# Gate products by rows of tokens: each contraction of 128 rows as two of 64, in two banks

## The chip, the cores and the metric

The kernel runs on one core of one Trainium2 chip. A core has a matrix engine (TensorE, PE in the profile, with its weight loads as PEld), a vector engine (VectorE, DVE), a scalar engine (ScalarE, ACT), GpSimd (POOL), and SyncE (SP), which issues most of the transfers. Products go into PSUM, whose banks hold 512 F32 numbers on each of 128 partitions; everything else lies in SBUF. The metric is the device time of one execution in microseconds. The kernel before takes 1186.93 us, the median of three runs (1186.53 to 1187.04).

## The reference

Two layers over 256 tokens of width 1024. Each has a SwiGLU block, a mixer, and a second SwiGLU block, all with a residual and a layer norm. The change is in the mixer, in the two gates; cut to that:

```python
def _mixer(x, layer, w_in, gate_b, ...):
    z = x @ w_in
    u, v, q, k, val, gates = jnp.split(z, SPLITS, axis=-1)
    h_a = _chunked_sgu(gelu(u), gelu(v), ...)
    h_b = _diff_attention(rope(q), rope(k), val, lam_full)      # with a norm behind it
    g = jax.nn.sigmoid(gates.reshape(bsz, seq, N_BRANCH, D_MODEL) + gate_b)
    m = g[:, :, 0] * (h_a @ w_branch[0]) + g[:, :, 1] * (h_b @ w_branch[1])
    return m @ w_out
```

For each branch the gate is a product of 256 tokens with a 1024 x 1024 matrix, plus a bias, through a sigmoid. Half of its columns (512) are made by rows of tokens, which is the part that changes; the other half by columns of the gate.

## The kernel before, in words

Precision. Inputs and weights are F32. Each product is made of three in a shorter form (fp32r): a number is split into hi and lo, and hi·hi, lo·hi and hi·lo are added up in a bank. ACT makes the hi of a weight (L195), DVE the lo (L197), in `stream`, which also fetches 1 MB of weights; buffers for hi and lo number eight each. `xh` and `xl` are the two parts of x, transposed, so that the contraction lies on the partitions: KT = 8 blocks of 128 rows.

A gate by rows of tokens (`gate_rows`, L1103) calls `gemm_b` (L324). That takes one bank for each half of the tokens (t = 0 and 1, 128 tokens each). With `tail=TAIL` = 8 all four weight pieces are held, and the products run t by t: for each t, eight blocks k, and for each the three products of `three` (L280, its matmuls are on L283): the weight load is a block of x (128 x 128), the moving operand 512 columns of the weight. That is 24 products for each t. When a t is through, `done` adds the bias into `gr` (DVE, L1109) and takes the tanh (ACT, L1110).

A gate by columns (`gate_columns`, L1114) and the q and k products (`rope`, L968) call `gemm_a2` (L285): two banks, eight products of 512 columns for each on L295, then eight of 256 columns for each on L302; ACT copies half of each bank (L303) and DVE adds the other half to it (L305, or L307 for q), which frees the bank.

Banks. PSUM is a pool of four "main" banks and four "side" banks. A main bank is taken from the four in turn, by `bank()`; a product into it waits until the last reader of its former content is through.

Order. TensorE's order is written out by hand: it executes exactly in the order of the code. The other engines' instructions are put in order by a scheduler that goes by priorities. Work beside the products (attention, norms) is a set of small tasks; `beat(w)` moves a clock on after so many products, and a task whose time has come adds its instructions there. So attention's products stand between those of the gates: the scores (`scores`, L1001, F32, with 64 rows each, in two banks in turn) and the product with the values (L1055 and L1057, F32, 128 rows). The scores pass through DVE (L1013) and ACT's exponential (L1015).

In each layer the order around the change is: q and k of four pairs of heads, gate rows of branch 0 (stage 1 below), gate columns of branch 0, gate rows of branch 1 (stage 2), gate columns of branch 1, and so on.

Of the kernel before, what the change touches and what calls it, by code (L numbers as in the profile page):

```python
# [17 lines left out]
ALU = mybir.AluOpType  # L18
AX = mybir.AxisListType

P = 128
D = 1024
T = 256
NT = T // P
KT = D // P
# [14 lines left out]
TAIL = 8  # L40
# [14 lines left out]
def trunk(ctx, tc, x, xT, w13a, w13b, w2, wb, wqk, wu, wg, wgr, wbr, wbrr, wo, gateb, gatebr, sgug, sgub, sguwT, sgubias, lam, diffg,  # L55
          lng, lnb, lngT, lnbT, cosT, sinT, out):
    nc = tc.nc
    V, A, G, PE = nc.vector, nc.scalar, nc.gpsimd, nc.tensor
# [15 lines left out]
    def name(s):  # L74
        serial[0] += 1
        return f"{s}_{serial[0]}"

    def bank():
        return psum.tile([P, 512], F32, tag="main", name=name("bank"))

    def side_bank():
        return psum.tile([P, 512], F32, tag="side", name=name("sbank"))

    def slots(s, n, dtype=F32):

        return [act.tile([P, 512], dtype, tag="slot", name=name(s)) for _ in range((n + 1) // 2)]
# [8 lines left out]
    def parts(f):  # L95
        return (lambda k: f(k)[:, :T]), (lambda k: f(k)[:, T:])
# [27 lines left out]
    def beat(w):  # L124

        clock[0] += w
        for task in list(tasks):
            if task[0] <= clock[0]:
                turn(task)

    def turn(task):
        try:
            task[0] = clock[0] + next(task[1])
        except StopIteration:
            tasks.remove(task)
# [10 lines left out]
    latest, added, emptied, silu, turned_by, loaded, spread = [None, None], [None], [None], [None], [None], [None], [None]  # L146
# [3 lines left out]
    def inline(eng, ins):  # L150
        if line[2]:
            line[eng is V] = ins
        return ins

    def behind(ins):

        return tc.issue_after(ins) if ins is not None else nullcontext()

    def fetch(src, width=CH, raw=None):

        step()
        if raw is None:
            raw = raw_pool.tile([P, CH], F32, tag="raw", name=name("raw"))
        for g in gate:
            g[0] -= 1
        while len(gate) > 1 and gate[1][0] < 0:
            gate.pop(0)
        with behind(gate[0][1] if gate and gate[0][0] < 0 else None):
            if isinstance(raw, list):
                for j, v in enumerate(raw):  # L170
                    loaded[0] = nc.sync.dma_start(v, src[:, j * HC : (j + 1) * HC]).ins
            else:
                loaded[0] = nc.sync.dma_start(raw[:, :width], src).ins
        return raw

    def stream(src, width=CH, sub=HC, lent=(), after=(None, None), pool=()):

        raw = fetch(src, width)  # L180
        out = []
        first = sooner.pop() if sooner else latest
        for o in range(0, width, HC):
            eng = G if o // HC in pool else V
            if o // HC in lent:
                hi, lo = ([act.tile([P, 512], F32R, tag="slot", name=name(n)) for _ in range(2)] for n in ("lhi", "llo"))
                at = [(hi[j], lo[j]) for j in range(2)]
            else:
                hi = hi_pool.tile([P, HC], F32R, tag="hi", name=name("whi"))
                lo = lo_pool.tile([P, HC], F32R, tag="lo", name=name("wlo"))  # L190
                at = [(hi[:, p : p + sub], lo[:, p : p + sub]) for p in range(0, HC, sub)]
            for p, (h, w) in zip(range(0, HC, sub), at):
                r = raw[:, o + p : o + p + sub]
                with behind(first[0]), behind(line[0]):
                    inline(A, A.activation(h, r, AF.Copy).ins)  # L195
                with behind(after[o // HC] or (first[1] if eng is V else None)), behind(line[1] if eng is V else None):
                    low = eng.tensor_tensor(out=w, in0=r, in1=h.bitcast(F32), op=ALU.subtract).ins  # L197
                if eng is V:
                    inline(V, low)
            out.append((hi, lo))  # L200
        return out
# [112 lines left out]
    def rows_b(ps, t, k0, piece, xh, xl, kts, c0=0, n=512, first=0):  # L314

        hi, lo = piece
        for j in range(2):
            k, o = k0 + j, j * 512 + c0
            wh, wl = (w[j][:, c0 : c0 + n] if isinstance(w, list) else w[:, o : o + n] for w in (hi, lo))
            three(ps[:, :n], xh(k)[:, t * P : (t + 1) * P], xl(k)[:, t * P : (t + 1) * P], wh, wl,  # L320
                  k == first, k == (first - 1) % kts)
        beat(n / 1024)

    def gemm_b(src, kts, xh, xl, done, tail=4, last=()):  # L324

        blocks = [[(bank(), c, n) for c, n in (last if t else ()) or ((0, 512),)] for t in range(NT)]
        held = []
        for c in range(0, kts, 4):
            nk = min(4, kts - c)
            for i, piece in enumerate(stream(src[:, c * 512 : (c + nk) * 512], nk * 512)):  # L330
                k = c + 2 * i
                if k >= kts - tail:
                    held.append((k, piece))
                    continue
                for t in range(NT):
                    for ps, o, n in blocks[t]:
                        rows_b(ps, t, k, piece, xh, xl, kts, o, n)
        for t in range(NT):
            for ps, o, n in blocks[t]:
                for k, piece in held:  # L340
                    rows_b(ps, t, k, piece, xh, xl, kts, o, n)
                done(t, ps[:, :n], o, n)

    def homes(pool, tag):
        return [pool.tile([P, HC], F32, tag=tag, name=name("home")) for _ in range(2)]
# [191 lines left out]
    b = side_bank()  # L537
# [47 lines left out]
    def bc_load(src, after):  # L585
        t = res.tile([P, D], F32, tag="bc", name=name("bc"), bufs=2)
        V.tensor_copy(t[:, :1], after)
        spread[0] = G.dma_start(t, src.partition_broadcast(P)).ins
        return t
# [363 lines left out]
    def mixer(l, i, norm):  # L953
        xh, xl = parts(both)
# [139 lines left out]
        for hp in range(HEADS // 2):  # L1094
# [3 lines left out]
            if hp == 1:  # L1098
                gbias = bc_load(gatebr[l], qT[:, :1])
# [3 lines left out]
        def gate_rows(br):  # L1103

            gr = [slots("gr", 2)[0] for _ in range(NT)]
            grow.append(gr)

            def done(t, ps, c, n):
                added[0] = V.tensor_tensor(out=gr[t], in0=ps, in1=gbias[:, br * 512 : (br + 1) * 512], op=ALU.add).ins  # L1109
                emptied[0] = A.activation(gr[t], gr[t], AF.Tanh, scale=0.5).ins  # L1110

            gemm_b(wgr[l, br, 0], KT, xh, xl, done, tail=TAIL)

        def gate_columns(br):  # L1114
            gt = slots("gate", KT // 2)
# [7 lines left out]
        for br in range(2):  # L1123
            gate_rows(br)
            gate_columns(br)
# [14 lines left out]
        for h in range(2):  # L1140
            def got_v(t, ps, c, n):
                A.activation(vg[t][:, h], ps, AF.Gelu)
                V.bn_stats(out=vst[t][:, h * 6 : h * 6 + 6], in_=vg[t][:, h])
            gemm_b(wb[l, V_, h], KT, xh, xl, got_v)
# [14 lines left out]
        for h in range(2):  # L1159
            s = slice(h * 512, h * 512 + 512)  # L1160
# [34 lines left out]
        def branch_rows(br, h):  # L1195
            def done(t, ps, c, n):
                g = grow[br][t]
                a = V.scalar_tensor_tensor(out=g, in0=g, scalar=1.0, in1=ps, op0=ALU.add, op1=ALU.mult)
                if br == 0:
                    a = V.tensor_tensor(out=g, in0=g, in1=grow[1][t], op=ALU.add)  # L1200
                    beside(turned(t, g, grow[1][t]), 0)
                added[0] = a.ins

            gemm_b(wbrr[l, br, 0], KT, lambda k: h[k][:, :T], lambda k: h[k][:, T:], done, tail=8)
# [137 lines left out]
```

## Time and profile before

| what | value |
|---|---|
| median of three runs | 1186.93 us |
| the profiled execution, own time | 1186.92 us |
| its span | 1185.2 us |
| TensorE's granted clock, mean | 1.0 |
| gate stages, layer 0: start, end | 250.15 to 262.41 us, 275.23 to 289.22 us |
| gate stages, layer 1: start, end | 836.56 to 848.83 us, 861.64 to 875.63 us |

The rows of the profile read like this. In the timeline a row is: start in us from the span's start, how long, engine, line, operation, output <- inputs, shapes (for PE rows x columns of the weights, then the moving operand), how often in a row, and in brackets idle time before it with what ended it. A product's listed length includes its way through the array, so lengths overlap; steps are read from starts. A row with "x8" covers eight products from the first start to the last end. A row of one line's or one tile's instructions has shortest/median/longest in ns. L numbers are lines of the kernel before, as printed above.

### The profile page before, as it was taken

To read this page: it belongs to the slowest core of one execution; us is meant where nothing else is said; L and a number is where in the kernel's file an instruction comes from. 1 tells how busy PE (TensorE), PEld (TensorE's weight loads), DVE (VectorE), ACT (ScalarE), POOL (GpSimd) and SP (SyncE) were. 2 spreads that over 40 slices of the span, in tenths; PEclk is the share of its full clock that TensorE was granted. 3 is DMA by queue.
4 is the path that set the end of the run, shared out by engine and by line. 5 is a ranking of instruction groups with operands and counts; after the bars stand their busy time and mean duration, and the time that the engine had idled before them with its cause. 6 is when DMAs were issued, how large, how long until landed. Compare 5 with 4: busy or idle time off the path is not lost.

```text
span 1185.2 us, 16670 instructions
## 1 busy us (share of the span) xinstructions
PE 1179.9 (100%) x5775; PEld 993.9 (84%) x5775; DVE 1012.7 (85%) x1562; ACT 827.7 (70%) x1417; POOL 287.1 (24%) x350
## 2 busy tenths in 40 slices
PE   9999999999999999999999999999999999999998
PEld 7888888888888888888888888888888888888887
DVE  6989989788688989889899889888975989988895
ACT  6688658559955677876667876576798556679761
POOL 1012201247420220051020171003564112102600
PEclk9999999999999999999999999999999999999999
DMA  9869976768865658689668699586666755786881
GB/s 355 261 203 262 288 273 209 262 194 236 247 208 170 227 190 272 186 275 275 231 222 263 191 278 274 201 290 226 212 213 205 254 182 170 253 251 206 274 258 36
DMA packets 129620, 275.10 MB, mean 232 GB/s; under 512 B 89040, under 2 KB 90368, under 8 KB 105472
## 3 DMA queue, kind: packets, MB, share of 16 engines
q1 hardware_dynamic: 121968, 248.67, 63.4%
q0 software_dynamic: 6992, 24.71, 8.7%
q8 instruction: 45, 0.74, 0.2%
q10 hardware_dynamic: 576, 0.66, 0.2%
q14 instruction: 39, 0.32, 0.1%
HBM read 248.05 MB, written 1.05 MB: 210 GB/s over the span
## 4 chain that ended last, share of the span: by engine, by line
PE 99%; DMA 0%; DVE 0%; ACT 0%; DVEq 0%; issue 0%
PE bank L283 46%; PE bank L295 15%; PE sbank L376 12%; PE bank L410 10%; PE bank L302 8%; PE sbank L410 3%; PE bank L527 2%; PE sbank L1001 1%; PE bank L376 1%; PE sbank L1057 1%; PE sbank L1175 1%; DMA xtok<-in_xT 0%; PE sbank L1055 0%; PE sbank L698 0%; DVE xtok L685 0%; DVE st L635 0%
## 5 line engine op out<-in xcount | busy, mean ns | idle before, releaser
L197 DVE TENSOR_TENSOR wlo<-raw,whi 128x1024 fp32r<-128x1024 f32 (+1 forms) x346 | 379.2, 1123 | 50.5 <-ACT whi L195 36.6
L195 ACT ACTIVATE whi<-raw 128x1024 fp32r<-128x1024 f32 (+1 forms) x350 | 323.4, 952 | 131.6 <-PE bank L283 42.7
L283 PE MATMUL bank<-whi,x 128*128 128x512 f32 x1224 | 386.3, 390 | 0.0
L283 PEld LDWEIGHTS bank<-whi,x 128*128 128x128 f32 x1224 | 229.8, 188 | 47.6
L283 PE MATMUL bank<-wlo,x 128*128 128x512 f32 x612 | 238.2, 389 | 0.0
L249 DVE TENSOR_TENSOR wlo<-raw,whi 128x1024 fp32r<-128x1024 f32 (+1 forms) x123 | 143.3, 1186 | 21.7 <-ACT whi L247 12.8
L247 ACT ACTIVATE whi<-raw 128x1024 fp32r<-128x1024 f32 (+1 forms) x123 | 121.1, 1002 | 53.7 <-DVE raw L359 24.8
L295 PE MATMUL bank<-x,whi 128*128 128x512 f32 x640 | 153.3, 391 | 0.0
L295 PEld LDWEIGHTS bank<-x,whi 128*128 128x128 f32 x640 | 118.2, 188 | 23.8
L283 PEld LDWEIGHTS bank<-wlo,x 128*128 128x128 f32 x612 | 114.9, 188 | 23.4
L229 POOL COPY seven<-seven 128x512 uint16<-128x512 uint16 x16 | 58.6, 3722 | 134.2 <-ACT whi L195 54.7
L302 PEld LDWEIGHTS bank<-x,wlo 128*128 128x128 f32 x640 | 81.4, 191 | 2.9
L302 PE MATMUL bank<-x,wlo 128*128 128x256 f32 x640 | 82.6, 283 | 0.0
L410 PE MATMUL bank<-whi,hhi 128*128 128x512 f32 (+1 forms) x182 | 68.2, 375 | 0.0
L410 PE MATMUL bank<-whi,hlo 128*128 128x512 f32 (+1 forms) x182 | 67.9, 373 | 0.0
L410 PE MATMUL bank<-wlo,hhi 128*128 128x512 f32 (+1 forms) x182 | 67.9, 373 | 0.0
L977 POOL TENSOR_TENSOR swap<-swap,sin_t 128x512 f32<-128x512 f32 x16 | 27.3, 1704 | 101.4 <-DMA swap<-z 69.7
L741 POOL COPY nvia<-ntwo 128x256 uint16<-128x256 uint16 x20 | 9.8, 539 | 162.2 <-DMA ntwo<-nvia 156.1
L303 ACT ACTIVATE r<-bank 128x256 f32<-128x256 f32 x96 | 34.8, 372 | 16.7 <-PE bank L302 16.7
L376 PE MATMUL sbank<-whi,xhs 128*128 128x512 f32 x128 | 42.0, 389 | 0.0
L359 DVE TENSOR_TENSOR raw<-raw,home 128x1024 f32<-128x1024 f32 x32 | 39.1, 1235 | 1.7 <-DMA home<-in_w13b 1.7
L410 PEld LDWEIGHTS bank<-whi,hlo 128*128 128x128 f32 x182 | 34.3, 188 | 6.1
(285 smaller groups left out, 2150.0 us busy)
## 6 DMA issues: line engine op xcount, KB each, us to landing
raw<-in_w13b SPq DMA_DIRECT2D x68, 1024.0 KB, 6.0
raw<-in_w SPq DMA_DIRECT2D x32, 1024.0 KB, 7.1
raw<-in_wb SPq DMA_DIRECT2D x16, 1024.0 KB, 6.0
raw<-in_wqk SPq DMA_DIRECT2D x16, 1024.0 KB, 6.4
home<-in_w13b SPq DMA_DIRECT2D x16, 512.0 KB, 5.9
raw<-in_w13a SPq DMA_DIRECT2D x8, 1024.0 KB, 4.9
home<-in_w SPq DMA_DIRECT2D x16, 512.0 KB, 4.2
raw<-in_wgr SPq DMA_DIRECT2D x8, 1024.0 KB, 5.3
```

The source lines that it names most:

```text
L195: inline(A, A.activation(h, r, AF.Copy).ins)
L197: low = eng.tensor_tensor(out=w, in0=r, in1=h.bitcast(F32), op=ALU.subtract).ins
L229: eng.tensor_copy(out=o, in_=i)
L247: a = A.activation(hi, src, AF.Copy).ins
L249: return a, eng.tensor_tensor(out=lo, in0=src, in1=hi.bitcast(F32), op=ALU.subtract).ins
L283: PE.matmul(ps, xx, w, start=start and n == 0, stop=stop and n == 2)
L295: PE.matmul(b[-1], hi[:, k * P : (k + 1) * P], xc(k), start=k == 0, stop=False)
L302: PE.matmul(b[n][:, :T], lo[:, k * P : (k + 1) * P], xc(k)[:, :T], start=False, stop=k == KT - 1)
L303: emptied[0] = A.activation(r[:, s], b[n][:, T:], AF.Copy, scale=scale).ins
L359: inline(V, V.tensor_tensor(out=v, in0=v, in1=m, op=ALU.add).ins)
L376: PE.matmul(ps, x[o](k), y, start=start and k == n == 0, stop=stop and k == 3 and n == 2, skip_group_check=True)
L410: PE.matmul(q[c][t][:, :n] if o == 0 else more[:, :n], x(k, t), y, start=k == 8 and m == 0 and (c, t) != (1, 0), stop=k == FT - 1 and m == ...
```

## The change

`gate_rows` calls a new function, `gemm_halves`, in place of `gemm_b`. Each product of 128 rows becomes two: rows 0-63 of x and of the weight go into one bank, rows 64-127 into another, one behind the other in TensorE's order. So a stage has four banks, two for each t, and 96 products in place of 48. DVE's `done` adds the bias to the first bank, then the second bank to that. The weights, their splits and the transfers are the same. (Blank lines at the head of the new function are left out.)

```diff
+    def gemm_halves(src, xh, xl, done):
+        ps = [[bank() for _ in range(2)] for _ in range(NT)]
+        held = [piece for c in range(0, KT, 4) for piece in stream(src[:, c * 512 : (c + 4) * 512])]
+        for t in range(NT):
+            for n, (hi, lo) in enumerate(held):
+                for j in range(2):
+                    k, s = 2 * n + j, slice(j * 512, (j + 1) * 512)
+                    xs_ = [x(k)[:, t * P : (t + 1) * P] for x in (xh, xl)]
+                    for m, (w, x) in enumerate(((hi, xs_[0]), (lo, xs_[0]), (hi, xs_[1]))):
+                        for half, b in enumerate(ps[t]):
+                            r = slice(half * P // 2, (half + 1) * P // 2)
+                            PE.matmul(b, x[r], w[r, s], start=k == m == 0, stop=k == KT - 1 and m == 2)
+                beat(0.5)
+            done(t, ps[t])
...
-            def done(t, ps, c, n):
-                added[0] = V.tensor_tensor(out=gr[t], in0=ps, in1=gbias[:, br * 512 : (br + 1) * 512], op=ALU.add).ins
+            def done(t, ps):
+                V.tensor_tensor(out=gr[t], in0=ps[0], in1=gbias[:, br * 512 : (br + 1) * 512], op=ALU.add)
+                added[0] = V.tensor_tensor(out=gr[t], in0=gr[t], in1=ps[1], op=ALU.add).ins
                 emptied[0] = A.activation(gr[t], gr[t], AF.Tanh, scale=0.5).ins
 
-            gemm_b(wgr[l, br, 0], KT, xh, xl, done, tail=TAIL)
+            gemm_halves(wgr[l, br, 0], xh, xl, done)
```

The order of instructions moves with it. TensorE, layer 0, stage 1, where t=0 ends and t=1 begins, before (buffer numbers are kept; banks are handed out in the order of these numbers, 2400 and 2445 being the last k product's, the two just ahead of the stage; what an instruction waits for is in brackets, DVE_49 being VectorE):

```order
L283 MATMUL bank_480_2494<-whi_490_2512,x_216_1213 128x512
L283 MATMUL bank_480_2494<-wlo_491_2513,x_216_1213 128x512
L283 MATMUL bank_480_2494<-whi_490_2512,x_216_1213 128x512 x2
L283 MATMUL bank_480_2494<-wlo_491_2513,x_216_1213 128x512
L283 MATMUL bank_480_2494<-whi_490_2512,x_216_1213 128x512
L283 MATMUL bank_481_2495<-whi_483_2498,x_215_1212 128x512 [waits DVE_49]
L283 MATMUL bank_481_2495<-wlo_484_2499,x_215_1212 128x512
```

and now:

```order
L360 MATMUL bank_480_2494<-whi_492_2514,x_216_1213 128x512
L360 MATMUL bank_481_2495<-whi_492_2514,x_216_1213 128x512
L360 MATMUL bank_482_2496<-whi_485_2500,x_215_1212 128x512 [waits DVE_49]
L360 MATMUL bank_483_2497<-whi_485_2500,x_215_1212 128x512 [waits DVE_49]
L360 MATMUL bank_482_2496<-wlo_486_2501,x_215_1212 128x512
L360 MATMUL bank_483_2497<-wlo_486_2501,x_215_1212 128x512
```

Before, t=0 and t=1 take the banks of the k product before the last (2341 and 2350), and the last k product's two go to the gate columns behind the stage. Now t=0 takes both of the former, and t=1 the two banks of the last k product, 2400 and 2445, whose reader on VectorE is the row z<-bank (L305). Elsewhere TensorE's order is the same, the visits of the attention included: L1055 and L1057 within t=1 of stage 1, and between t=0 and t=1 of stage 2; the scores (L1001) in the middle of t=1 of stage 2.

VectorE in the same place, before (z is the k product's sum, qk its rotated form, gr the gate):

```order
L305 TENSOR_TENSOR z_472_2455<-bank_470_2445,r_471_2454 128x256 [waits Activation_49]
L1032 RECIPROCAL rc_461_2412<-sums_459_2410 128x4
L197 TENSOR_TENSOR wlo_531_2715<-raw_527_2708,whi_530_2714 128x1024
L1033 SCALAR_TENSOR_TENSOR c_460_2411<-rc_461_2412,neg_lam0_1894,sums_459_2410 128x4 [waits DVE_49]
L1024 SCALAR_TENSOR_TENSOR d_473_2479<-pp_467_2430,c_460_2411,pp_466_2425 128x256 [waits DVE_49]
L1024 SCALAR_TENSOR_TENSOR d_473_2479<-pp_467_2430,c_460_2411,pp_466_2425 128x256
L1024 SCALAR_TENSOR_TENSOR d_474_2480<-pp_469_2440,c_460_2411,pp_468_2435 128x128 x2
L976 TENSOR_TENSOR qk_477_2487<-z_472_2455,cos_t_137 128x512
L1109 TENSOR_TENSOR gr_478_2492<-bank_480_2494,bc_403_2165 128x512 [waits DMASW7_49,PE_49]
L981 TENSOR_TENSOR qk_477_2487<-qk_477_2487,swap_476_2486 128x512 [waits DMAHW4_49,DMAHW5_49,DVE_49,Pool_49]
```

and now:

```order
L996 TENSOR_TENSOR qk_477_2487<-z_472_2455,cos_t_137 128x512
L1001 TENSOR_TENSOR qk_477_2487<-qk_477_2487,swap_476_2486 128x512 [waits DMAHW4_49,DMAHW5_49,DVE_49,Pool_49]
L1129 TENSOR_TENSOR gr_478_2492<-bank_480_2494,bc_403_2165 128x512 [waits DMASW7_49,PE_49]
L1130 TENSOR_TENSOR gr_478_2492<-gr_478_2492,bank_481_2495 128x512 [waits DVE_49,PE_49]
L197 TENSOR_TENSOR wlo_549_2834<-raw_547_2831,whi_548_2833 128x1024 [waits DMAHW3_49,Activation_49]
L197 TENSOR_TENSOR wlo_551_2838<-raw_547_2831,whi_550_2837 128x1024 [waits Activation_49]
```

The rows up to the first qk row are the same as before. The two adds of t=0 stand behind the second qk row, where the one add stood ahead of it. In stage 2 two weight splits on VectorE stand further ahead, one of them before the scores' rows and one between the two adds of t=1; the rest of VectorE's order is the same, and ScalarE's, GpSimd's and SyncE's differ in a place or two each in stage 2 or not at all.

## The prediction, as it was put on record

> **What bounds the kernel now.** I read the page's busy times and its chain first, then TensorE's own list of waits.
>
> ```profile
> PE 1179.9 (100%) x5775; PEld 993.9 (84%) x5775; DVE 1012.7 (85%) x1562; ACT 827.7 (70%) x1417; POOL 287.1 (24%) x350
> PE 99%; DMA 0%; DVE 0%; ACT 0%; DVEq 0%; issue 0%
> PE sbank L539 <- DVE warm L535: 1.1, 1, 1.1
> PE sbank L677 <- ACT minus L675: 0.7, 1, 0.7
> PE bank L527 <- ACT x L247: 0.3, 1, 0.3
> ```
>
> TensorE (PE) is the bound from end to end: 99% of the chain is PE, and its waits are three, 2.1 us in all (columns: us in total, times, longest), none of them near the gates. So what the change adds to PE's sequence goes straight into the time, and a new wait of PE is paid in full: there is no other wait that it could replace. What counts is the step from one product to the next, read from starts in the timeline of the first gate stage (layer 0, branch 0):
>
> ```profile
> 252.45 0.39 PE L283 MATMUL bank<-wlo,x 128*128 128x512 f32 x1
> 252.67 0.61 PE L283 MATMUL bank<-whi,x 128*128 128x512 f32 x2
> 253.13 0.39 PE L283 MATMUL bank<-wlo,x 128*128 128x512 f32 x1
> ```
>
> Three products in 0.68 us are 0.2267 us each, though each is listed as 0.39 (they overlap). A gate stage is 48 of them, 24 for each half of the tokens (t=0, then t=1), and there are four stages, two in each layer: 192 products, which become 192 pairs.
>
> **The pair itself: 0, with bounds.** The kernel already has pairs of 64 rows in two banks: the attention's scores (L1001, F32).
>
> ```profile
> 226.67 0.60 PE L1001 MATMUL sbank<-qk,qk 64*128 64x256 f32 x4
> 226.89 0.60 PE L1001 MATMUL sbank<-qk,qk 64*128 64x256 f32 x4
> 227.10 0.60 PE L1001 MATMUL sbank<-qk,qk 64*128 64x256 f32 x6
> 227.32 0.50 PE L1001 MATMUL sbank<-qk,qk 64*128 64x128 f32 x6
> 259.70 0.38 PE L1055 MATMUL sbank<-val,d 128*128 128x128 f32 x2
> 259.92 0.61 PE L1057 MATMUL sbank<-val,aT 128*128 128x128 f32 x4
> 260.37 0.39 PE L1055 MATMUL sbank<-val,d 128*128 128x128 f32 x2
> ```
>
> Pairs of 256 columns start every 0.217 us (226.67 to 227.32 in three steps), 0.108 per 128 columns. Full-height F32 products of 128 columns take 0.112 (0.45 us for the four from 259.92 to 260.37). So two halves side by side cost one whole product: they do run together, and they gain nothing either, because the columns still pass one after another. The gates' products are of the faster form (fp32r), for which no pair is in the trace. Its bounds: 256 columns take 0.1195 (1.91 us for the sixteen L302 rows below, 248.24 to 250.15), so 512 columns are 0.2145 and 0.012 is a gap per product (2 x 0.1195 - 0.2267). If the pair loses the gap it steps by 0.2145, if it has it twice by 0.239. I take 0.2267, since the F32 rows show a pair stepping like a single product.
>
> **Passing between heights: +2.3 us.**
>
> ```profile
> 242.85 2.00 PE L295 MATMUL bank<-x,whi 128*128 128x512 f32 x8
> 244.78 1.58 PE L1001 MATMUL sbank<-qk,qk 64*128 64x256 f32 x16
> 246.29 2.11 PE L295 MATMUL bank<-x,whi 128*128 128x512 f32 x8
> 248.24 2.08 PE L302 MATMUL bank<-x,wlo 128*128 128x256 f32 x16
> 250.15 0.40 PE L283 MATMUL bank<-whi,x 128*128 128x512 f32 x1
> 260.95 0.48 PE L283 MATMUL bank<-whi,x 128*128 128x512 f32 x1
> 262.41 0.39 PE L295 MATMUL bank<-x,whi 128*128 128x512 f32 x1
> ```
>
> Around one visit to 64 rows: eight products take 1.93 instead of 8 x 0.2267 = 1.81, the scores 1.51 instead of 4 x 0.217 + 4 x 0.108 = 1.30, the next eight 1.95 instead of 1.81. That is 0.12 + 0.21 + 0.14 = 0.47, say 0.23 each way. The visit to L1055/L1057, F32 at full height, costs nothing: its twelve products take 1.25 (259.70 to 260.95; 12 x 0.112 = 1.34) and the six behind 1.46 (6 x 0.2267 = 1.36). So the price belongs to the height, not to the type. The Trainium skill (TensorEngine Tiling (Array Packing), Key Properties) says that a change of the tiling mode, though not of the tile, drains TensorE. The trace agrees, by the 0.47; without that rule the sum below would be 2.8.
>
> Passages per layer in the new order: in (stage 1), out and in around L1055/L1057, out; in (stage 2), out and in around L1055/L1057, out: 8. The scores inside stage 2 now stand among 64-row pairs, so their 2 passages go. The first "in" is swallowed by the wait below. 8 - 2 - 1 = 5, times 0.23, times 2 layers = 2.3. Bounds: 0 if fp32r hides them, 3.5 if each is half as dear again.
>
> **The bank wait: +2.8 us.** Four accumulating banks are handed out in turn. Before, a stage took two; the two behind them stayed with the last q/k product (L295/L302) until VectorE (DVE) had read them. Now t=1 needs exactly those two, and the DVE row that frees the second stands at:
>
> ```profile
> 255.42 0.39 ACT L1015 ACTIVATE pp<-pp,mx 128x128 f32<-128x128 f32 x1
> 255.81 0.36 ACT L303 ACTIVATE r<-bank 128x256 f32<-128x256 f32 x1
> 256.07 1.04 ACT L195 ACTIVATE whi<-raw 128x1024 fp32r<-128x1024 f32 x1
> 257.02 0.35 ACT L303 ACTIVATE r<-bank 128x256 f32<-128x256 f32 x1
> 257.41 0.42 DVE L305 TENSOR_TENSOR z<-bank,r 128x256 f32<-128x256 f32 x1 [0.19 <-ACT r L303]
> 255.39 0.61 PE L283 MATMUL bank<-whi,x 128*128 128x512 f32 x2
> 836.56 0.40 PE L283 MATMUL bank<-whi,x 128*128 128x512 f32 x1
> 841.80 0.62 PE L283 MATMUL bank<-whi,x 128*128 128x512 f32 x2
> 842.18 0.42 DVE L305 TENSOR_TENSOR z<-bank,r 128x256 f32<-128x256 f32 x1 [0.19 <-ACT r L303]
> ```
>
> Layer 0: t=1 starts at 255.62 (second product of the 255.39 row, 5.47 after 250.15); the bank is free at 257.41 + 0.42 = 257.83: PE is 2.21 late. Layer 1: start 842.03, bank free 842.60: 0.57. Together 2.8. Nothing in the change moves that DVE row: it waits for ScalarE (ACT), whose copy stands behind the softmax exponentials (L1015) and a weight split, all fed before the stage. PE is in order, so while it waits all products of t=1 and the whole rest stand behind it. A slower or faster t=0 changes nothing here while it ends before the bank is free.
>
> In the second stage of a layer t=1 takes the banks of the gate columns before it, and these are read (L305, gz) long before; after the first wait PE is later still.
>
> **The adds on DVE: 0.** Eight more adds; the nearest row, the first add, has 0.684 each:
>
> ```profile
> L1109 DVE TENSOR_TENSOR gr<-bank,bc x8: 677/684/692, 261.1 to 876.5; 128x512 f32<-128x512 f32 x8
> 262.39 1.07 DVE L981 TENSOR_TENSOR qk<-qk,swap 128x512 f32<-128x512 f32 x1 [0.59 <-POOL swap L977]
> 847.15 1.07 DVE L981 TENSOR_TENSOR qk<-qk,swap 128x512 f32<-128x512 f32 x1 [0.57 <-POOL swap L977]
> 848.83 1.52 PE L295 MATMUL bank<-x,whi 128*128 128x512 f32 x6
> ```
>
> What hides them is PE's new lateness. The gate columns behind stage 1 take t=0's banks, and both adds of t=0 now stand behind the q/k add: in layer 1 they free the first bank at 847.15 + 1.07 + 0.68 = 848.90 and the second at 849.58. PE wants the first at 848.83 + 0.57 + 0.46 + 0.23 = 850.09: 1.2 us of cover (layer 0: 264.14 against 262.41 + 2.21 + 0.69 = 265.31, also 1.2). Without it, the first add alone would cost up to 0.7 a layer.
>
> **Sum:** 0 + 2.3 + 2.8 + 0 = +5.1 us on the profiled execution, whose own time is 1186.92 (span 1185.2 and 1.7 around it); the median is 1186.93. Forecast **1192.0**. With the pair's bounds on the 144 products that no wait covers (24 + 48 per layer): 144 x 0.012 = 1.7 either way, and about 1.1 for the passages: 1189 to 1195.
>
> **Rivals.** (1) The halves share a way to the banks. In the F32 rows each half delivers a column in twice the time that an fp32r product needs (0.217 for 256 columns against 0.2267 for 512), so two full-rate streams side by side have not been seen. If they took turns altogether, a pair would be 0.4533: 192 x 0.2267 = 43.5, the bank wait gone (t=0 ends late enough), 6 passages a layer, 2.8: 1233. If a pair were a tenth dearer, 0.249: 144 x 0.0227 = 3.3, and t=0 in layer 1 ends 0.2 past its bank: 1195.5. Against it: F32 pairs show no trace of sharing. The Trainium skill (TensorE: Matmul & The Clock Gate, Measured speedup vs the span model) has 3.07 instead of 4 for four row tiles of 512 columns; as an estimate from that, two would cost about 1.1 of one, the second of these cases. No run here shows it yet.
>
> (2) Not slower: the banks are free in time. The place is the DVE row of the last q/k product, the price 2.8. It decides from the point where that row ends before 255.8 in layer 0, 2 us sooner; between the layers its lead over PE does differ by 1.6 (7.68 after the stage's start against 6.04). Then two more "in" are paid: 5.1 - 2.8 + 0.5 = 2.8 at 0.2267 a pair, 0.5 with the gap lost on all 192 (-2.3). Middle: 1.7, 1188.6. Against it: nothing upstream changes.
>
> (3) Faster would need a pair under 0.2145 - the columns forbid that - or waits that I do not see in PE's list.
>
> **Numbers.** Forecast 0.74, rival 1 0.13, rival 2 0.08, faster 0.05. This kernel's measurement tells 0.2% (2.4 us) from no change; so slower 0.87, same 0.08, faster 0.05. The range runs from rival 2's middle, 1188.5, to 1196.5, past the tenth-dearer pair; it leaves out the serial pair and the faster cases.
>
> **What will show it.** Two starts 5 to 10 ns apart in each pair and 0.227 between pairs; a PE wait of some 2.2 us at 255.6 with DVE z as its releaser, and of 0.3 to 0.6 in layer 1; products at each change of height some 0.1 us late; no PE wait at the gate columns. Pairs of 0.45, no wait at t=1, or a wait for the gr adds would prove me wrong.

## The result, and the profile after

| | before | after |
|---|---|---|
| median | 1186.73 us (1186.46 to 1187.04, 4 runs) | 1194.58 us (1194.31 to 1195.86, 4 runs) |
| ratio, 95% interval | | 1.0067 (1.0054 to 1.0079) |
| profiled execution, own time and span | 1186.92 us, 1185.2 us | 1194.31 us, 1192.6 us |
| granted clock, mean | 1.0 | 1.0 |

The change costs 7.85 us by the medians and 7.4 by the two spans. The page after the change, its busy times and its chain's first line:

```profile
PE 1184.5 (99%) x5967; PEld 995.5 (83%) x5967; DVE 1016.2 (85%) x1570; ACT 828.0 (69%) x1417; POOL 285.4 (24%) x350
PE 92%; DVE 3%; ACT 2%; issue 1%; POOL 1%; DMA 0%; SPq 0%; DVEq 0%; POOLq 0%; ACTq 0%
```

TensorE is nearly as full as before (99% of the span busy against 100%), and still only 92% of the chain is TensorE, where it was 99%: 5% now runs through VectorE and ScalarE. So somewhere TensorE waits for a chain of those two. TensorE's own list of waits says where (us in total, times, longest):

```profile
PE sbank L1075 <- ACT d L1069: 1.8, 2, 0.9
PE bank L360 <- DVE z L305: 1.3, 2, 0.7
PE sbank L559 <- DVE warm L555: 1.0, 1, 1.0
PE sbank L697 <- ACT minus L695: 0.7, 1, 0.7
```

The last two are those of before (1.1 and 0.7). The second is the bank wait, as forecast. The first is new and in no term of the prediction: the values product (L1075, before L1055) waits for ScalarE's d.

How much each place costs is read by taking the same product of TensorE in both traces and subtracting the starts. Where this difference grows, time is lost. It is -0.20 us ahead of the first gate stage (the heads of the two executions differ by that) and 7.43 at the end, so the change loses 7.63:

| stretch | layer 0 | layer 1 |
|---|---|---|
| stage 1 | 2.91 | 0.81 |
| stage 2 and up to the values product in the u part | 0.86 | 0.65 |
| the values product in the u part | 1.13 | 1.14 |
| what is left, up to the next layer or the end | 0.11 | 0.02 |

TensorE's timeline of the changed kernel where t=1 of stage 1 begins in layer 0, with VectorE's rows that free the two banks:

```profile
254.71 0.62 PE L360 MATMUL bank<-whi,x 64*128 64x512 f32 x4
255.16 0.39 PE L360 MATMUL bank<-wlo,x 64*128 64x512 f32 x2
255.39 0.39 PE L360 MATMUL bank<-whi,x 64*128 64x512 f32 x2
256.37 0.50 PE L360 MATMUL bank<-whi,x 64*128 64x512 f32 x1 [0.60 <-DVE z L305]
257.59 0.50 PE L360 MATMUL bank<-whi,x 64*128 64x512 f32 x1 [0.72 <-DVE z L305]
...
255.89 0.42 DVE L305 TENSOR_TENSOR z<-bank,r 128x256 f32<-128x256 f32 x1 [0.79 <-ACT r L303]
257.11 0.42 DVE L305 TENSOR_TENSOR z<-bank,r 128x256 f32<-128x256 f32 x1 [0.19 <-ACT r L303]
```

From 254.71 three pairs take 0.68 us: 0.2267 a pair, the step of a whole product. The two of a pair start 3 to 4 ns apart (255.389 and 255.393 in the trace). Then the first half of t=1 starts when the first bank is free (255.89 + 0.42) and the second 1.2 us later, when the second one is (257.11 + 0.42): in layer 0 the wait is at the place, with the releaser and of the size that was forecast. In layer 1 there is none. The same place there, t=1 beginning in the row of 846.81:

```profile
846.16 0.42 DVE L305 TENSOR_TENSOR z<-bank,r 128x256 f32<-128x256 f32 x1 [0.19 <-ACT r L303]
846.81 0.62 PE L360 MATMUL bank<-whi,x 64*128 64x512 f32 x4
```

The second bank is free at 846.16 + 0.42 = 846.58, 0.45 us before TensorE needs it (the second pair of that row starts at 847.03).

### The profile page after: what moved, and what is told of

It reads as the page before. It is cut to its first block, busy times and chain, and to the rows that moved or that the text cites. A ratio compares the mean times of both kernels' runs of the same rounds, so it can differ in the third digit from the quotient of the medians.

```text
span 1192.6 us, 17064 instructions
## 1 busy us (share of the span) xinstructions
PE 1184.5 (99%) x5967; PEld 995.5 (83%) x5967; DVE 1016.2 (85%) x1570; ACT 828.0 (69%) x1417; POOL 285.4 (24%) x350
## 4 chain that ended last, share of the span: by engine, by line
PE 92%; DVE 3%; ACT 2%; issue 1%; POOL 1%; DMA 0%; SPq 0%; DVEq 0%; POOLq 0%; ACTq 0%
PE bank L283 42%; PE sbank L396 12%; PE bank L295 12%; PE bank L430 10%; PE bank L302 6%; PE sbank L430 3%; PE bank L360 2%; PE bank L547 2%; DVE wlo L197 1%; ACT pp L1035 1%; PE bank L396 1%; PE sbank L1077 1%; PE sbank L1196 1%; POOL swap L997 1%; PE sbank L1021 1%
## 5 line engine op out<-in xcount | busy, mean ns | idle before, releaser
L283 PE MATMUL bank<-whi,x 128*128 128x512 f32 x1096 | 344.7, 389 | 0.0
L283 PEld LDWEIGHTS bank<-whi,x 128*128 128x128 f32 x1096 | 205.7, 188 | 42.9
L283 PE MATMUL bank<-wlo,x 128*128 128x512 f32 x548 | 213.2, 389 | 0.0
L283 PEld LDWEIGHTS bank<-wlo,x 128*128 128x128 f32 x548 | 102.9, 188 | 21.0
L229 POOL COPY seven<-seven 128x512 uint16<-128x512 uint16 x16 | 64.7, 4107 | 128.3 <-ACT whi L195 81.7
L360 PE MATMUL bank<-whi,x 64*128 64x512 f32 x256 | 44.3, 396 | 1.3 <-DVE z L305 1.3
```

Of the source, the lines that this page charges most:

```text
L229: eng.tensor_copy(out=o, in_=i)
L283: PE.matmul(ps, xx, w, start=start and n == 0, stop=stop and n == 2)
L360: PE.matmul(b, x[r], w[r, s], start=k == m == 0, stop=k == KT - 1 and m == 2)
```

## The experiments

All times are medians, beside those of the kernel before on the same chip; the ratio is that to before, with its 95% interval. Line numbers move a little from kernel to kernel. Losses told "in starts" are read from one profiled execution beside the one of before; its head, ahead of the first gate stage, can be 0.1 to 0.5 us shorter or longer than that of before, so their sums differ from the medians by about as much. The diffs are cut to the lines that matter.

### Halves in one stage alone

Two kernels: branch 0 (stage 1) alone, and branch 1 (stage 2) alone. `whole` is `done` as it was before the change, with one add.

```diff
-            gemm_halves(wgr[l, br, 0], xh, xl, done)
+            if br == 0:                     # br == 1 in the second kernel
+                gemm_halves(wgr[l, br, 0], xh, xl, done)
+            else:
+                gemm_b(wgr[l, br, 0], KT, xh, xl, whole, tail=TAIL)
```

Stage 1 alone:

> Halves in branch 0 alone (stage 1 of each layer); branch 1 computes its gate rows as before, with whole products. Theory A (the time of the change is the bank wait, the passages between heights and, apart from both, work that was put into another order on VectorE and ScalarE around stage 2): here the order on ScalarE, GpSimd and SyncE is that of before and VectorE has only the four adds of branch 0 more, so the bank wait (1.2 and 2.2 us seen in layer 0, 0.3 to 0.6 in layer 1) and the passages of stage 1 are all that is left: +3.9 us, the lead that the changed kernel's TensorE had lost at the start of stage 2 (3.02 + 0.92), 1190.9; no TensorE wait for d at the values product. Rival B (the wait of about 1.06 us a layer for ScalarE's d at the values product comes from stage 1 being late): the wait is there and the time is +6.0, 1193.

1191.66 us against 1187.17, ratio 1.0042 (1.0030 to 1.0055): 4.5 more. There is no wait for d, so B is out. But A's 3.9 is not the whole of it either. TensorE's waits have a new line, in layer 1 (the first line here; behind it VectorE's and ScalarE's timeline of this kernel):

```profile
PE bank L283 <- DVE gz L305: 0.7, 1, 0.7
...
850.28 1.07 DVE L1001 TENSOR_TENSOR qk<-qk,swap 128x512 f32<-128x512 f32 x1 [2.33 <-POOL swap L997]
854.38 3.50 DVE L197 TENSOR_TENSOR wlo<-raw,whi 128x1024 fp32r<-128x1024 f32 x3 [1.65 <-ACT whi L195]
852.77 0.63 ACT L1131 ACTIVATE gr<-gr 128x512 f32<-128x512 f32 x1 [6.63 <-DVE gr L1130]
```

The same tanh before the change:

```profile
846.62 0.63 ACT L1110 ACTIVATE gr<-gr 128x512 f32<-128x512 f32 x1 [2.43 <-DVE gr L1109]
```

TensorE is 3.1 us later here than before, and ScalarE's tanh 6.15. It idles 6.63 us, since VectorE comes to the gate adds only behind the q/k add, and that one waits for GpSimd. Behind the tanh in ScalarE's queue stand the weight splits, behind these the scores' rows and the copies out of the gate columns' banks. In starts of the same products, stage 2 of layer 1 loses 1.03 us.

Stage 2 alone:

> Halves in branch 1 alone (stage 2 of each layer); stage 1 as before. The VectorE and ScalarE order around stage 2 is that of the changed kernel (weight splits ahead of the scores' rows and between the adds). Theory A (moved splits make ScalarE's d late): no bank wait, passages +1.3 us (0.75 + 0.53), and the wait for d at the values product, about 1.06 us in each layer, with its full size: +3.4, 1190.3. Rival B (stage 1's lateness makes it): no wait for d, +1.3, 1188.2.

1190.72 us against 1187.17, ratio 1.0032 (1.0019 to 1.0044): 3.55 more, A's 3.4. The wait for d is there in its full size, with stage 1 as it was:

```profile
PE sbank L1075 <- ACT d L1069: 1.8, 2, 0.9
```

So it belongs to stage 2 and not to the lateness out of stage 1.

### Two banks without halves, and halves without a second bank

Whole products of 128 rows, even blocks k into one bank, odd ones into the other:

```diff
-                        for half, b in enumerate(ps[t]):
-                            r = slice(half * P // 2, (half + 1) * P // 2)
-                            PE.matmul(b, x[r], w[r, s], start=k == m == 0, stop=k == KT - 1 and m == 2)
+                        PE.matmul(ps[t][j], x, w[:, s], start=n == m == 0, stop=n == KT // 2 - 1 and m == 2)
```

> Whole products of 128 rows, but still two banks for each half of the tokens (even pieces of the contraction into one, odd ones into the other) and both adds on VectorE; no change of height, so what it leaves out is the split into 64 rows alone. Theory A: the bank wait stays, 2.2 us in layer 0 and about 0.6 in layer 1, and the passages are gone: +2.8, 1189.7; on VectorE no weight split stands ahead of the scores' rows here, so the wait for d should be gone or small. Rival B (the second add, or stage 1's lateness, makes the wait for d): it stays, 1.06 a layer, +4.9, 1191.8. Rival C (the bank wait belongs to pairs): +0 to +0.3.

1188.70 us against 1187.17, ratio 1.0015 (1.0006 to 1.0024): 1.5 more, not 2.8. There are no waits for d, and the bank wait is there, but smaller. TensorE's timeline of this kernel:

```profile
255.03 0.39 PE L358 MATMUL bank<-whi,x 128*128 128x512 f32 x1
256.12 0.50 PE L358 MATMUL bank<-whi,x 128*128 128x512 f32 x1 [0.70 <-DVE z L305]
256.45 0.39 PE L358 MATMUL bank<-wlo,x 128*128 128x512 f32 x1
256.68 0.40 PE L358 MATMUL bank<-whi,x 128*128 128x512 f32 x1
257.33 0.50 PE L358 MATMUL bank<-whi,x 128*128 128x512 f32 x1 [0.25 <-DVE z L305]
```

Three products go into the first bank ahead of the first one into the second, so the second bank is needed 3 x 0.2267 = 0.68 us later than by a pair. In layer 0 the wait costs 1.6 instead of 2.1, in layer 1 nothing; 0.5 more goes into a wait for gz at the head of stage 2 of layer 0 (in starts, 2.1 together; this execution's head was 0.4 us shorter than that of before). I had left those three products out of my 2.8. The wait itself is one for two banks a half, with or without pairs, so C is out.

Rows 0 to 63 alone, in one bank and with the first add alone, so that half of the gates' sum is left out:

```diff
-        ps = [[bank() for _ in range(2)] for _ in range(NT)]
+        ps = [[bank()] for _ in range(NT)]
...
-                        for half, b in enumerate(ps[t]):
-                            r = slice(half * P // 2, (half + 1) * P // 2)
-                            PE.matmul(b, x[r], w[r, s], start=k == m == 0, stop=k == KT - 1 and m == 2)
+                        PE.matmul(ps[t][0], x[:64], w[:64, s], start=k == m == 0, stop=k == KT - 1 and m == 2)
```

> Only rows 0 to 63 of every piece of the contraction, into one bank as before, with one add: half of the gates' sum is left out. The order on every engine is that of before, there is no second bank, and so no bank wait and no wait for d. Theory A: a lone product of 64 rows steps by 0.2267 us like a whole one, and what is left is the price of the passages: 8 a layer less the 2 of the scores inside stage 2, so 6 x 0.23 x 2 = +2.8, 1189.7. Rival B (a change of height costs nothing for fp32r, what was seen belongs to the pairs): within 0.3 of before. Rival C (a product of 64 rows is faster): under before, 0.012 x 192 = -2.3 at the most if its gap goes.

1189.44 us against 1187.17, ratio 1.0020 (1.0011 to 1.0029): 2.3 more. From the first gate stage on, TensorE's starts fall back by 2.63, which is 12 passages at 0.22. The steps (timeline of this kernel):

```profile
250.94 0.39 PE L358 MATMUL bank<-wlo,x 64*128 64x512 f32 x1
251.17 0.61 PE L358 MATMUL bank<-whi,x 64*128 64x512 f32 x2
251.63 0.39 PE L358 MATMUL bank<-wlo,x 64*128 64x512 f32 x1
```

Three products of half the height in 0.69 us: they step like whole ones, and what they cost is the passage. A holds, B and C do not.

### The pairs not alternated

```diff
-                for j in range(2):
-                    ...
-                        for half, b in enumerate(ps[t]):
+                for half, b in enumerate(ps[t]):
+                    r = slice(half * P // 2, (half + 1) * P // 2)
+                    for j in range(2):
+                        ...
```

> The pairs are not alternated: within each piece of the weights (two k, six products) all six products of rows 0 to 63 stand first, then all six of rows 64 to 127. Same products, same banks. Theory A (two halves run side by side only where products of the two row groups stand next to each other in TensorE's order): products of one group run one after another at 0.2267 us, only those at the seams overlap, so 40 us or more longer, some 1185 + 43 = 1228 to 1230, with no bank wait. Rival B (TensorE runs ahead and finds the other group's work): as the changed kernel, 1194.6.

One run: 1196.16 us against 1187.06, 9.1 more where A had some 43. A is wrong; B's mechanism holds, at 1.6 us over its number. The stage begins like this (timeline of this kernel):

```profile
249.91 0.50 PE L360 MATMUL bank<-whi,x 64*128 64x512 f32 x1
250.25 0.39 PE L360 MATMUL bank<-wlo,x 64*128 64x512 f32 x1
250.48 0.62 PE L360 MATMUL bank<-whi,x 64*128 64x512 f32 x3
250.82 0.51 PE L360 MATMUL bank<-wlo,x 64*128 64x512 f32 x2
```

Two products run alone, 0.34 and 0.23 us apart. Then, at 250.48, there are two starts within 6 ns, and from there starts come at first at about 0.115 us, two streams of one product each 0.23 us. The second of those two is listed with 0.493 us, as the first product behind a change of height or a wait is: it is the first one into the second bank. The six of the first row group are not through by then: three of them still stand ahead in TensorE's order. So TensorE starts products of the other row group ahead of those that wait for their own. What the order costs is the stream that runs alone at the head and the end of each t; that is not 0 (each stage loses more than in the changed kernel, in starts 1.9 to 3.4 us against 0.65 to 2.9), but a small part of 43.

### The order on VectorE and ScalarE

Now the changed kernel with one thing undone that nobody wrote into the diff, the new order around stage 2. The two weight splits that had moved forward are held behind the last row of the scores and the last d (`held_back` keeps these two rows, and `stream` gets them as `after`):

```diff
+                wait = ((None, held_back[0]), (held_back[1], held_back[1]))[gp] if gp < 2 else (None, None)
-                (_, uu), = gemm_a2([wu[l, gp]], both, lambda m: uu)
+                (_, uu), = gemm_a2([wu[l, gp]], both, lambda m: uu, after=wait)
```

> The changed kernel with one thing more: two weight splits of the u part are held behind the last row of the scores and behind the last d of the attention, so that the order on VectorE in stage 2 is that of before with the four second adds put in; SyncE's order is that of before again, ScalarE's differs in a few places. Theory A (the wait for d at the values product comes from splits put ahead of the scores and between the adds): that wait is gone in both layers, 2.13 us less, 1192.4; since layer 1 is then less late by 1.06, the wait for gz that the halves in stage 1 alone had (1.03 us, from the adds standing behind the q/k add) can come back in layer 1 in part, at most to 1193.4. Rival B (the extra adds themselves make it, whatever the order): the wait stays, 1194.6.

1192.35 us against 1187.06, ratio 1.0042 (1.0029 to 1.0055): 5.3 more instead of 7.85, as A had it. The wait for d is gone from TensorE's list, and the wait for gz did not come. This is what the order does in stage 2 of layer 0. The timeline of the changed kernel, VectorE, ScalarE, TensorE:

```profile
289.00 2.36 DVE L197 TENSOR_TENSOR wlo<-raw,whi 128x1024 fp32r<-128x1024 f32 x2 [3.68 <-ACT whi L195]
...
296.34 1.23 DVE L197 TENSOR_TENSOR wlo<-raw,whi 128x1024 fp32r<-128x1024 f32 x1 [2.76 <-ACT whi L195]
297.49 0.68 DVE L1129 TENSOR_TENSOR gr<-bank,bc 128x512 f32<-128x512 f32 x1
298.09 1.22 DVE L197 TENSOR_TENSOR wlo<-raw,whi 128x1024 fp32r<-128x1024 f32 x1
299.22 0.68 DVE L1130 TENSOR_TENSOR gr<-gr,bank 128x512 f32<-128x512 f32 x1
...
291.74 0.51 ACT L1035 ACTIVATE pp<-pp,mx 128x256 f32<-128x256 f32 x1 [1.82 <-DVE mx L1033]
299.93 0.63 ACT L1131 ACTIVATE gr<-gr 128x512 f32<-128x512 f32 x1 [1.63 <-DVE gr L1130]
305.86 0.79 ACT L1069 ACTIVATE d<-d 128x256 uint16<-128x256 uint16 x2
...
306.80 0.46 PE L1075 MATMUL sbank<-val,d 128*128 128x128 f32 x2 [0.89 <-ACT d L1069]
```

The same rows before the change:

```profile
285.64 1.23 DVE L197 TENSOR_TENSOR wlo<-raw,whi 128x1024 fp32r<-128x1024 f32 x1 [4.05 <-ACT whi L195]
287.25 0.51 ACT L1015 ACTIVATE pp<-pp,mx 128x256 f32<-128x256 f32 x1 [0.69 <-DVE mx L1013]
291.73 0.61 ACT L1110 ACTIVATE gr<-gr 128x512 f32<-128x512 f32 x1
299.23 0.81 ACT L1049 ACTIVATE d<-d 128x256 uint16<-128x256 uint16 x2
302.17 0.38 PE L1055 MATMUL sbank<-val,d 128*128 128x128 f32 x2
```

And with the order restored:

```profile
296.72 0.61 ACT L1133 ACTIVATE gr<-gr 128x512 f32<-128x512 f32 x1
303.37 0.81 ACT L1071 ACTIVATE d<-d 128x256 uint16<-128x256 uint16 x2
```

Read it from the top. One split ahead of the scores' rows became two (x1, x2): ScalarE's exponentials, 3.36 us late by VectorE's first split already, are 4.49 late. VectorE then pays for that lateness: the split ahead of the adds of t=1 waits 2.76 us for a hi part which ScalarE makes only behind the late exponentials. Another split stands between the two adds, and ScalarE's tanh, 8.2 us later than before, makes the queue behind it idle for 1.63. In the end d is 6.63 us later, at a TensorE that is 3.6 later; its slack before was 302.17 - 300.04 = 2.1 (the values product's start less d's end), and 6.63 - 3.6 - 2.1 = 0.9 is what TensorE waits (0.89 in its row; the starts there fall back by 1.1 in all). The edit also puts SyncE's order back and holds both splits at once. No run separates these, but ScalarE's idle times on this way, from the exponentials to d, end on VectorE alone.

Next, the wait for gz of the kernel with stage 1 alone. The last q/k add is put behind the two gate adds of t=0 (the third argument is how much later, in the time of `beat`, the rest of `rope` is added):

```diff
-            kT = rope(wqk[l, hp, 1], 1.0)
+            kT = rope(wqk[l, hp, 1], 1.0, 2.05 if hp == HEADS // 2 - 1 else 1.55)
```

> The kernel with halves in stage 1 alone, and the last q/k add put behind the two gate adds of t=0, as VectorE had it before the change; nothing else moves on any engine. Theory A (in layer 1 the gate adds stood behind the q/k add, which waits 2.33 us for GpSimd; ScalarE's tanh waited for them, the weight splits for ScalarE, the scores' rows for the splits, and TensorE 1.03 us for the gate columns' bank): the wait for gz in layer 1 is gone, 1190.6. Rival B (the second adds and the late halves themselves push VectorE, the order is of no account): 1191.7 stays.

1190.71 us against 1187.06, ratio 1.0029 (1.0018 to 1.0040), A's 1190.6. The loss of 1.03 in layer 1 is gone, and the tanh (timeline) stands 3.4 us sooner than in the kernel without this edit:

```profile
849.36 0.63 ACT L1131 ACTIVATE gr<-gr 128x512 f32<-128x512 f32 x1 [3.23 <-DVE gr L1130]
```

Both orders restored in the changed kernel:

> The changed kernel with both orders of before restored: the u part's splits held back as in the run before the last, and the last q/k add behind the gate adds of t=0. Theory A: nothing but the bank wait and the passages is left, as the changed kernel's TensorE shows them up to the values product (layer 0: 3.77, layer 1: 1.45; 5.2 in all), so 1192.2, with no wait for d nor for gz. Rival B (layer 1's lead, now smaller, is eaten by another wait): up to 1193.4. Rival C (orders are of no account): 1194.6.

1192.35 us against 1187.06, ratio 1.0042 (1.0029 to 1.0056), 5.3 more. No new wait but the one for the banks is left. From the first gate stage on TensorE loses 4.77 in starts: 2.77 in passages and 2.0 in the bank wait, which is counted from behind the first "in" and with the 0.2 that the second half, one product behind the first, runs alone at the end of t=1. The q/k order adds nothing to stage 2's order that the medians show: in the changed kernel TensorE is late enough in layer 1 for the gate adds to be where they are. It removes only a wait of 0.2 for gz at the head of stage 2 of layer 0.

### The bank wait

One weight split on ScalarE, which stood between the two copies of the last q/k product, moved behind them:

```diff
-                with behind(first[0]), behind(line[0]):
+                with behind(first[0]), behind(line[0]), behind(last_copy[1] if o else None):
```

> The kernel with both orders restored, and one weight split on ScalarE (the second half of the second gate-column piece) moved from between the two copies of the last q/k product to behind them; its partner on VectorE moves with it. Theory A (the bank wait of t=1 lasts until ScalarE's second copy and VectorE's add behind it; the split ahead of that copy is 1.05 us of it): the second bank comes free about 0.95 us sooner in both layers, which takes 0.95 from layer 0's wait and the whole wait of layer 1, some 0.4: 1.3 less than the run before, 1191.0. Rival B (another thing holds t=1): 1192.35 as before. Rival C (the split now comes too late for the gate columns): over 1192.35, with a TensorE wait for whi or wlo.

1191.94 us against 1186.88, ratio 1.0041 (1.0027 to 1.0054): 5.1 more against 5.3, which these runs do not tell apart. The timeline of this kernel tells why it is so little:

```profile
255.70 0.36 ACT L304 ACTIVATE r<-bank 128x256 f32<-128x256 f32 x1
256.07 0.68 DVE L1002 TENSOR_TENSOR qk<-qk,swap 128x512 f32<-128x512 f32 x1
256.67 0.42 DVE L306 TENSOR_TENSOR z<-bank,r 128x256 f32<-128x256 f32 x1
```

ScalarE's copy is 1 us sooner, but VectorE has a q/k add in hand until 256.67, so the bank is free only 0.28 us sooner (7.67 after the q/k add that begins this chain, at 249.00, against 7.94 in the changed kernel: 257.11 less 249.17). In layer 1 there was no wait left to take. A named a true cause and overlooked the next one in VectorE's queue.

## Why the prediction was right, and where it was not

The forecast was 1192.0 and the time 1194.58: slower, by the mechanisms named, and within the range. The sum was 5.1; the kernel with both orders restored, which has nothing but the terms of that sum, has 5.3. The other 2.5 us have a cause that the prediction gave no price. That 1194.58 still lies in the range is in part luck: the upper end, 1196.5, was there for pairs a tenth dearer, which did not come, and not for this.

- **The pair itself, 0.** Right. 0.2267 us a pair, 3 to 4 ns between its two starts (forecast 5 to 10). Rival 1 falls: no time is lost to a shared way. The loss that the Trainium skill (TensorE: Matmul & The Clock Gate, Measured speedup vs the span model) has for four tiles is not there for two of 64 rows.
- **Passages, 2.3.** Right in price, 0.22 each in the kernel with rows 0 to 63 alone, where nothing else is in the way. That agrees with the drain that the Trainium skill (TensorEngine Tiling (Array Packing), Key Properties) names. In layer 0 the first "in", 0.19, is swallowed as forecast, since VectorE's row sets the end of the wait; in layer 1 there is no wait to swallow it. So eleven are paid and not ten. The 2.77 above counts the swallowed one too, and its wait is shorter by as much.
- **The bank wait, 2.8.** The mechanism, place and releaser are right; the size is right in layer 0 (2.1 behind the first "in", 2.3 with it, forecast 2.2) and wrong in layer 1 (0, forecast 0.57). There TensorE comes 5.0 us later than before and the banks are free only 4.0 later (VectorE's second z starts at 846.16 against 842.18): the step had let both be late alike, though the chain to z runs from a transfer through GpSimd and VectorE (GpSimd's row ahead of it is 3.95 later, 828.85 against 824.90) and not with TensorE. So rival 2 holds for layer 1 and not for layer 0.
- **The adds on DVE, 0.** This is the step that failed. It asked only when VectorE would free a bank for TensorE, found 1.2 us of cover, and stopped there. Not asked was who else stands behind the adds: ScalarE's tanh, and behind that, in the same queue, splits, exponentials and d. Nor were the moved splits of stage 2 priced, though the order showed them: one ahead of the scores' rows, one between the adds (why the scheduler put them forward stays open). They cost 2.5 us: with stage 2's order restored TensorE loses 5.73 instead of 7.63, though its bank wait in layer 0 happened to be 0.64 longer (the chain to z began 0.58 later in that execution), so 1.90 + 0.64. Of this, 2.27 stands at the values product itself. And the cover is not a constant: with halves in stage 1 alone, TensorE less late, the two adds of t=0, behind the q/k add, cost 1.03.
- **What will show it.** The step between pairs, the wait at t=1 of layer 0 and the lateness at each change of height came as said; the wait of 0.3 to 0.6 in layer 1 did not. No PE wait at the gate columns: right for the changed kernel but for 0.2 us in stage 2, wrong as soon as stage 1 stands alone.

None of these kernels beats the kernel before, and with a pair that steps like a whole product a gain would have to come from elsewhere.

## What to carry to other kernels

A contraction cut into row groups gained nothing on TensorE here, where the whole height was in use; it pays for each change of height, here 0.22 us, and needs twice as many banks at the same moment. When work is added to an engine that has time to spare, follow its whole queue and the queue of whoever waits for it, up to the next wait of the bounding engine: the price is in what stands behind, and it can be taken back by restoring the order alone, here 2.5 of 7.6 us. An order that a scheduler makes is part of the change: rows that move in it need a price like those in the diff.

## What the runs showed of the hardware that was not expected

In one run TensorE did not hold products of two row groups to the program's order, though the prediction has "PE is in order": with six products of one group ahead of six of the other, the second group began 0.58 us after the first (250.489 against 249.909), with three of the first group's six not yet started, and both went on side by side. A product that waits for a bank does hold up those behind it: in the changed kernel the first bank of t=1 was free at 256.31, but its second product started only at 257.59, with the first one into the second bank. So the prediction's step from a late bank to a late TensorE stands.

A lone product of 64 rows, 512 columns, steps at 0.23 us like one of 128 rows. The first product behind a change of height or a wait is listed with 0.49 to 0.50 us instead of 0.39, and the next one starts 0.33 after it instead of 0.23: some 0.1 us of each passage is there.
